# Where a fast matrix product's sums are made: on GpSimd beside the up projection, or on VectorE in other stages

## The chip, the cores and the metric

The kernel runs on one core of a Trainium2 chip. The metric is the device time of one execution in microseconds (us). A core has TensorE (PE, matmuls; its weight loads are shown as PEld), VectorE (DVE), ScalarE (ACT), GpSimd (POOL) and SyncE (SP), whose queue issues all of this kernel's DMAs.

## The reference, cut to what matters

One decoder layer over 16 + 1024 tokens of width 1024: a token mixer (latent attention and a Mamba-2 state-space mixer, gated and summed), then a gated MLP; each is followed by a layer norm.

```python
mixed = sigmoid(g_attn) * y_attn + sigmoid(g_ssd) * y_ssd
h = layer_norm(ALPHA * h + mixed @ w_out, ln1_g, ln1_b)
u = causal_dwconv(h @ w_up, conv_w, conv_b)      # width 3; D_FF = 2816
gate, val = split(u, 2)
h = layer_norm(ALPHA * h + (silu(gate) * val) @ w_down, ln2_g, ln2_b)
```

All inputs and the output are float32.

## The kernel before, in words

Every matrix product is made of three matmuls in a rounded float32 format: an operand is split into a high part (a cast on ACT) and a low part (a subtraction on DVE, `split`, or the same two lines in `load_w`), and high x high, low x high and high x low are accumulated in PSUM. Weights come by DMA into `wraw` (two buffers of 512 KB) and are split into `wh` and `wl` (four buffers each in the pool that all stages share).

The stages that count here, in order of time:

- **Gates' stage** (pool `B3`, lines 666 to 762, about 540 to 720 us): 8 rounds; round m makes the attention's gate m (`gate`, with a DVE multiplication) and the attention's output projection (`o_proj`, ACT copies PSUM). In between lie `dt_chain` and `h_centered`, small work, mostly on DVE.
- **State-space mixer**, then the mixer's projections and `wout` for two halves of the tokens (514 columns each). The second half's sum of squares `ssq` ends this part.
- **Root**: `inv_root` (line 201) sums `ssq` over the partitions with ten matmuls against ones, makes the reciprocal root in a chain of twelve small DVE operations, and spreads the result with ten matmuls against the identity. With it, `normed` (line 996) normalises the second half, stores it, and lines 1052 to 1075 make the seven right-hand forms of the next stage: sums and differences of the two halves, each split.
- **Up projection** (lines 1078 to 1238): the product h @ w_up is cut 2 x 2, and each block f of 128 gate and 128 value columns (`NFF` = 22 blocks) takes seven products of a Strassen-Winograd scheme instead of eight; a product is 24 matmuls in `mm3h`. `wload` brings two weight tiles per block, `wrest` makes the sums s1 to s4 of their quarters on POOL and splits them. `conv_up` is the width-3 convolution on ACT and DVE. Products 1 and 2 need only the first half of the tokens, which is ready long before; so for the first four blocks (`NHEAD`) these "tops" are made first, while the second half is normalised. They need rhs 1 and 2, and the others need the forms: 6 needs T2, 7 T3, 5 T1, 3 B2, 4 T4.
- **`down_sums`** (line 1178): for the same scheme in the next stage, four sums of the quarters of w_down are needed. For each of 11 pairs of weight rows it loads two 512 KB tiles, makes four subtractions on POOL in place, and stores both tiles to DRAM (`t13_d`, `t42_d`). It is called in the loop over blocks 4 to 14, its tiles have one buffer each, and it reads nothing but an input.
- **Down projection** (lines 1242 to 1392): seven products of 132 matmuls with 512 columns, over 11 values of j. The left sides are tiles A11, A12, A21, A22 of the gated values, loaded back from DRAM; `left` makes the sums of products 7, 6, 5 and 3 on POOL, per j, when `forms` asks for that j. `forms` splits the left and the right side; seven sets of buffers hold what is split ahead. Products come in the order 1, 2, 7, 6, 5, 3, 4.

The order of instructions on each engine is fixed ahead of time by a list planner, which takes of the instructions that it reckons ready the one that stands first in the program; `tc.high_priority(n)` lets a block count as n instructions earlier, and `tc.issue_after(ins)` makes the block's instructions on the same engine queue behind `ins`. On the chip each engine runs its list in that order, and SP issues its DMAs in order, each when its semaphores allow it.

Of the kernel before, what the change touches and what calls it, by code (L numbers as in the profile page):

```python
# [103 lines left out]
def tile_hybrid(ctx: ExitStack, tc: tile.TileContext, x, vecs, consts, cos, sin, win, wqb, wk, wv,  # L104
# [79 lines left out]
    def mm3h(ps, lhs, rhs, start=True):  # L184

        n = len(lhs)
        for k in range(n):
            (ah, al), (bh, bl) = lhs[k], rhs[k]
            for i, (a, b) in enumerate(((ah, bh), (al, bh), (ah, bl))):
                for c0, c1 in HC:  # L190
                    nc.tensor.matmul(ps[:, PO + c0:PO + c1], a, b[:, c0:c1], start=(start and k == 0 and i == 0),  # L191
                                     stop=(k == n - 1 and i == 2), skip_group_check=not start)

    def half(ps):
        return ps[:, PO:PO + HN]
# [2 lines left out]
        nc.scalar.copy(H, src)  # L198
        nc.vector.tensor_sub(L, src, f32(H))  # L199

    def inv_root(ss, n, scale, eps):


        ps = ctile() if n <= 512 else dpair()
        groups = [(0, n)] if n <= 512 else HC
        starts = [a + min(j * P, b - a - P) for a, b in groups for j in range(-(-(b - a) // P))]
        k = len(starts)
        for j, o in enumerate(starts):
            nc.tensor.matmul(ps[:, j:j + 1], ss[:, o:o + P], ones[:, :1], start=True, stop=True)
# [6 lines left out]
        for j, o in enumerate(starts):  # L216
            e = o + P
            nc.tensor.matmul(res[:, done:e], r[:, j:j + 1].broadcast_to([P, P]), ident[:, done - o:],
                             start=True, stop=True)
            done = e  # L220
        return res

    def rsqrt_cols(r, v, t):
# [442 lines left out]
    with pool("B3", 1) as p3:  # L666
# [24 lines left out]
        def dt_chain():  # L691
# [5 lines left out]
            for c in range(3):  # L697
# [27 lines left out]
                for k in range(3):  # L725
                    nc.tensor.transpose(tp[:S, k * 64:(k + 1) * 64], q[:, k * S:(k + 1) * S], ident[:64, :64])
                nc.scalar.copy(tok[:, 3 * c:3 * c + 3, :], tp[:S, :192].rearrange("p (a b) -> p a b", b=64))
        def h_centered(c):

            n = C1[c] - lo(c)  # L730
            hfs = []
            for k in range(KT):
                hfs.append(p3.tile([P, 352], F32, name="hf", tag="hf", bufs=9))
                nc.sync.dma_start(hfs[k][:, :n], h_d[k][:, lo(c):C1[c]])
            sum_ = p3.tile([P, 352], F32, name="hs", tag="hf", bufs=9)
            for k in range(1, KT):
# [18 lines left out]
        for m in range(KT):  # L755
            gate(B_GA, m, m1_d, yat)
            if m == 2:
                dt_chain()
            if m > 2 and m - 3 < 3:
                h_centered(m - 3)  # L760
            if m + 3 < KT:
                o_proj(m + 3)
# [284 lines left out]
    pf2 = eF.enter_context(pool("F2", 40))  # L1047
    p0 = eF.enter_context(pool("E0", 1))
    pz = eD.enter_context(pool("Dz", hB, "right"))
    with tc.high_priority(400):  # L1050
        rd = inv_root(ssq, HN, 1.0 / D, LN_EPS)
    T1, T2, T3, T4, B2 = ([None] * hB for _ in range(5))
    b11 = []
    for j in range(hB):
        b11.append(ftile(pz, F32))
        nc.sync.dma_start(b11[-1], h1_d[j][:, cols(0)])
    t2 = []
    for j in range(hB):
        b12, b22 = normed(1, j, rs[j], rd), normed(1, j + hB, rs[j + hB], rd)
        nc.vector.tensor_sub(b11[j], b12, b11[j])  # L1060
        t2.append(dtmp("t2", "yl" if j < 3 else "ml", 3))
        nc.vector.tensor_sub(t2[j], b22, b11[j])
        T2[j] = form(pf2, t2[j])
    for j in range(hB):
        nc.vector.tensor_sub(rs[j], rs[j + hB], rs[j])
        T3[j] = form(pf2, rs[j])
    for j in range(hB):
        T1[j] = form(pf2, b11[j])
    for j in range(hB):
        B2[j] = form(pf2, rs[j + hB])  # L1070
    for j in range(hB):
        b21 = dtmp("b21", "r", 8)
        nc.sync.dma_start(b21, h1_d[j + hB][:, cols(0)])
        nc.gpsimd.tensor_sub(b21, b21, t2[j])
        T4[j] = form(pf2, b21)

    rhs = {1: B1[:hB], 2: B1[hB:], 3: B2, 4: T4, 5: T1, 6: T2, 7: T3}
    HW = hB * P

    def wsplit(pl, src, bufs):
# [15 lines left out]

    def wrest(f, w):

        with tc.high_priority(wprio[0]):
            a11, a12 = wload(f)
            a21, a22 = wload(f + NFF)

            s1, s2, s3, s4 = (p0.tile([P, 512], F32, name=k, tag=k) for k in ("s1", "s2", "s3", "s4"))
            nc.gpsimd.tensor_add(s1, a21, a22)
            nc.gpsimd.tensor_sub(s2, s1, a11)  # L1110
            nc.gpsimd.tensor_sub(s3, a11, a21)
            nc.gpsimd.tensor_sub(s4, a12, s2)
            r = {}
            if w is None:
                r.update({1: wsplit(wp, a11, 4), 2: wsplit(wp, a12, 4)})
            for q, a in ((4, a22), (7, s3), (6, s2), (5, s1), (3, s4)):
                r[q] = wsplit(p0, a, 4) if q in (7, 6, 3) else wsplit(pe[0], a, 3)
            return r

    def prod(ps, q, w, start=True):  # L1120
        mm3h(ps, w[q], rhs[q], start)

    pe = []

# [35 lines left out]
        st[f]["c11"] = etile("c11", NHEAD)  # L1160
        nc.scalar.copy(st[f]["c11"], half(st[f]["x0"]))

    for f in range(NHEAD):
        with tc.high_priority(300):
            tops[f] = wtop(f)
            q = st[f]
            q["x0"] = dpair()
            prod(q["x0"], 1, tops[f])
            q["p1"] = etile("p1", NHEAD)
            nc.scalar.copy(q["p1"], half(q["x0"]))  # L1170
            if f:
                second(f - 1)
            if f == NHEAD - 1:
                second(f)

    eD.close()
    pe.append(eF.enter_context(pool("E1", 1)))
    def down_sums(j):

        x, y = (pe[0].tile([P, D], F32, name=k, tag=k) for k in ("tw1", "tw2"))  # L1180
        nc.sync.dma_start(x, wdl[j])
        nc.sync.dma_start(y, wdl[j + KH])
        (b11, b12), (b21, b22) = ((t[:, :512], t[:, 512:]) for t in (x, y))
        nc.gpsimd.tensor_sub(b11, b12, b11)
        nc.gpsimd.tensor_sub(b12, b22, b12)
        nc.gpsimd.tensor_sub(b22, b22, b11)
        nc.gpsimd.tensor_sub(b21, b21, b22)
        nc.sync.dma_start(t13_d[j], x)
        nc.sync.dma_start(t42_d[j], y)

    first(0)
    begun = 1
    for f in range(NFF):
        q = st[f]
        if f >= NHEAD and f < NHEAD + KH:
            down_sums(f - NHEAD)
        while begun < min(NHEAD, f + 2):
            first(begun)
            begun += 1
# [43 lines left out]
    with pool("Er", 4) as pr, pool("Ea", 4) as pa_, pool("Eh0", 8) as ph0, pool("Eb", 40) as pb, \  # L1243
# [10 lines left out]
            return raw[i, j]  # L1254

        def left(q, j):
            if q in (1, 2, 4):
                return A({1: 11, 2: 12, 4: 22}[q], j)
            if q == 7:
                t = p.tile([P, 512], F32, name="s3", tag="s3", bufs=3)  # L1260
                nc.gpsimd.tensor_sub(t, A(11, j), A(21, j))
                return t
            if q == 6:
                nc.gpsimd.tensor_add(A(21, j), A(21, j), A(22, j))
                nc.gpsimd.tensor_sub(A(11, j), A(21, j), A(11, j))
                return A(11, j)
            if q == 5:
                return A(21, j)
            nc.gpsimd.tensor_sub(A(12, j), A(12, j), A(11, j))
            return A(12, j)  # L1270
# [91 lines left out]
        for t in range(4):  # L1362
            add(t)
            nc.scalar.copy(u4[t], rp[t])
        product(1, x0, True, None, lambda t: nc.scalar.copy(p1[t], x0[t]))
        g2 = p.tile([P, D], F32, name="g2")
        b2 = p.tile([P, D], F32, name="b2")
        nc.sync.dma_start(g2, ln2[0:1].broadcast_to([P, D]))
# [1 line left out]

        x1 = banks(ctile)
        add = residual(0, 0, x1, True)
        product(2, x1, False, add, lambda t: nc.vector.tensor_add(p1[t], p1[t], x1[t]))
        x2 = banks(ctile)
        product(7, x2, True)
        product(6, x0, False, None, lambda t: nc.scalar.copy(u2[t], x0[t]))

        def c22(t):
            nc.vector.tensor_add(u4[t], u4[t], x0[t])
            nc.vector.tensor_add(u4[t], u4[t], x2[t])  # L1380
            nc.vector.bn_stats(bs[1][t][:, 1], u4[t])

        product(5, x0, False, None, c22)
        add = residual(0, 1, x0, False)
        product(3, x0, False, add, lambda t: norm2(0, t, (p1[t], x0[t]), (), (0, 1)))
# [104 lines left out]
```

## Time and profile before

| | us |
|---|---|
| runs | 2536.19, 2531.0, 2533.59 |
| median | 2533.59 |
| profiled execution, its own time | 2531.04 |
| its span, first to last instruction | 2529.3 |
| PE busy | 2403.9 (95%) |
| DVE busy | 1745.5 (69%) |
| ACT busy | 1136.7 (45%) |
| POOL busy | 336.8 (13%) |
| mean granted clock of PE | 0.977 |

Busy times of PE come from modelled ends, so a busy PE isn't always PE at its peak; the number of matmuls in a stretch is the surer measure. In a window's row there stand the stretch and its length, then for each engine the busy time and in brackets the count of instructions, the granted clock as a share of full speed, the share of DMA engines busy and the GB/s. A row of waits names who waited, at which line, for whom, the total, how often, and the longest. A row of the timeline gives start, duration, engine, line, operation, tiles, count, and in brackets the idle time before it and who ended it.

### The profile page before, as it was taken

The numbers are of one execution on the slowest core, as the hardware profiler recorded it, in microseconds if no ns is written. First come the engines' busy times: TensorE is split into PE (matmuls) and PEld (weight loads), VectorE is DVE, ScalarE is ACT, GpSimd is POOL, SyncE is SP. The second block draws the span as 40 slices with busy tenths as digits, with TensorE's granted clock in tenths as the row PEclk, the third lists the DMA queues.
The fourth block names the chain that finished last, engine by engine and source line by source line (L and its number), as shares of the span: only waits on it lengthen the run. The fifth ranks groups of instructions, "written<-read, shape, count | busy, mean of one in ns | idle before, by whom it ended". The sixth has DMA issues, their size and how long they took to land.

```text
span 2529.3 us, 42622 instructions
## 1 busy us (share of the span) xinstructions
PE 2403.9 (95%) x16319; PEld 2269.6 (90%) x16319; DVE 1745.5 (69%) x3857; ACT 1136.7 (45%) x2481; POOL 336.8 (13%) x278
## 2 busy tenths in 40 slices
PE   6999999999999999999999999998787999998896
PEld 6999899899999999999999999998787999997685
DVE  6467677684666777777777548547786777766558
ACT  6345455562245554555454323424433444444243
POOL 0000000000000000000000002011675222205504
PEclk9999999999999999999999999999798999999998
DMA  5121011152643212222221536543455222246232
GB/s 200 46 65 40 30 37 42 40 156 81 192 154 100 89 62 97 68 79 86 68 92 55 175 132 191 174 147 130 158 201 198 77 81 86 77 163 235 77 109 96
DMA packets 124620, 277.29 MB, mean 110 GB/s; under 512 B 14720, under 2 KB 49792, under 8 KB 122368
## 3 DMA queue, kind: packets, MB, share of 16 engines
q1 hardware_dynamic: 124416, 274.57, 33.0%
q8 instruction: 128, 2.10, 0.3%
q14 instruction: 76, 0.62, 0.1%
HBM read 209.62 MB, written 62.80 MB: 108 GB/s over the span
## 4 chain that ended last, share of the span: by engine, by line
PE 78%; DVE 7%; POOL 4%; DMA 4%; issue 3%; ACT 2%; SPq 0%; DVEq 0%; POOLq 0%; ACTq 0%
PE d L191 21%; PE g L171 12%; PE g L173 12%; PE g L172 12%; PE g L1321 5%; PE c L607 3%; PE c L882 2%; PE c L906 1%; PE c L601 1%; PE c L886 1%; DMA yl<-y_d 1%; DMA tw<-wdl 1%; DVE f L199 1%; PE c L554 1%; PE c L556 1%
## 5 line engine op out<-in xcount | busy, mean ns | idle before, releaser
L191 PE MATMUL d<-f,wh 128*128 128x258 f32 (+1 forms) x4000 | 666.5, 289 | 44.5 <-ACT u L1219 9.1
L191 PEld LDWEIGHTS d<-f,wh 128*128 128x128 f32 x4000 | 569.1, 196 | 49.6 <-ACT wh L198 10.3
L171 PE MATMUL g<-h,wh 128*128 128x348 f32 (+3 forms) x1560 | 507.5, 325 | 4.7 <-ACT lat L389 4.7
L173 PE MATMUL g<-h,wh 128*128 128x348 f32 (+3 forms) x1560 | 506.3, 325 | 0.0
L172 PE MATMUL g<-h,wl 128*128 128x348 f32 (+3 forms) x1560 | 506.1, 325 | 0.0
L191 PE MATMUL d<-f,wl 128*128 128x258 f32 (+1 forms) x2000 | 412.0, 289 | 5.2 <-DVE wl L199 3.6
L191 PEld LDWEIGHTS d<-f,wl 128*128 128x128 f32 x2000 | 319.6, 196 | 6.6 <-DVE wl L199 4.4
L161 DVE TENSOR_TENSOR wl<-wraw,wh 128x512 fp32r<-128x512 f32 (+2 forms) x278 | 193.7, 698 | 161.9 <-ACT wh L160 159.2
L171 PEld LDWEIGHTS g<-h,wh 128*128 128x128 f32 x1560 | 294.7, 189 | 7.6 <-ACT lat L389 5.0
L172 PEld LDWEIGHTS g<-h,wl 128*128 128x128 f32 x1560 | 295.0, 189 | 2.5 <-issue 2.4
L173 PEld LDWEIGHTS g<-h,wh 128*128 128x128 f32 x1560 | 294.3, 189 | 2.4 <-issue 2.4
L160 ACT CAST wh<-wraw 128x512 fp32r<-128x512 f32 (+2 forms) x278 | 167.3, 605 | 252.8 <-PE d L191 126.5
L199 DVE TENSOR_TENSOR wl<-wraw,wh 128x512 fp32r<-128x512 f32 x136 | 119.0, 884 | 74.3 <-ACT wh L198 74.3
L171 PE MATMUL g<-a,wh 128*128 128x348 f32 (+2 forms) x456 | 148.8, 327 | 1.6 <-DVE kn L199 1.1
L172 PE MATMUL g<-a,wl 128*128 128x348 f32 (+2 forms) x456 | 147.3, 323 | 0.0
L173 PE MATMUL g<-a,wh 128*128 128x348 f32 (+2 forms) x456 | 147.2, 323 | 0.0
L198 ACT CAST wh<-wraw 128x512 fp32r<-128x512 f32 x136 | 82.4, 618 | 120.6 <-DMA wraw<-wup 60.5
L787 DVE SCALAR_TENSOR_TENSOR xc<-g,V,xc 128x347 f32<-128x347 f32 (+2 forms) x180 | 103.7, 576 | 38.9 <-ACT xc L783 36.0
L1134 DVE SCALAR_TENSOR_TENSOR va<-u,V,va 128x512 f32<-128x512 f32 x88 | 99.9, 1135 | 20.9 <-ACT va L1132 19.5
L1321 PE MATMUL g<-wh,dh 128*128 128x512 f32 x352 | 112.4, 401 | 1.5 <-ACT wh L198 1.5
L872 ACT ACTIVATE G<-ac,tok 116x116 f32<-116x116 f32 x288 | 91.8, 380 | 42.7 <-PE c L882 42.7
L793 POOL MEMSET xc<- 128x4 f32 x20 | 2.0, 102 | 787.2 <-DVE y L919 454.1
(308 smaller groups left out, 4389.0 us busy)
## 6 DMA issues: line engine op xcount, KB each, us to landing
wraw<-win SPq DMA_DIRECT2D x65, 512.0 KB, 3.4
wraw<-wup SPq DMA_DIRECT2D x48, 512.0 KB, 3.7
ac<-cs_d SPq DMA_DIRECT2D x16, 1044.0 KB, 5.8
wraw<-wos SPq DMA_DIRECT2D x32, 512.0 KB, 3.9
tw<-wdl SPq DMA_DIRECT2D x22, 512.0 KB, 4.1
t_d<-tw SPq DMA_DIRECT2D x22, 512.0 KB, 2.8
gv<-gv_d SPq DMA_DIRECT2D x44, 256.0 KB, 5.6
wraw<-t_d SPq DMA_DIRECT2D x44, 256.0 KB, 3.2
```

The source lines that it names most:

```text
L160: nc.scalar.copy(h[:, :n * ncol], r)
L161: nc.vector.tensor_sub(l[:, :n * ncol], r, f32(h[:, :n * ncol]))
L171: nc.tensor.matmul(ps, ah, bh, start=(k == 0), stop=False)
L172: nc.tensor.matmul(ps, al, bh, start=False, stop=False)
L173: nc.tensor.matmul(ps, ah, bl, start=False, stop=(k == n - 1))
L191: nc.tensor.matmul(ps[:, PO + c0:PO + c1], a, b[:, c0:c1], start=(start and k == 0 and i == 0), stop=(k == n - 1 and i == 2), skip_group_c ...
L198: nc.scalar.copy(H, src)
L199: nc.vector.tensor_sub(L, src, f32(H))
L787: nc.vector.scalar_tensor_tensor(t[:, l:n], ps[:, hal + l - s:hal + n - s], vec("cw", (3 - s) * 24 + ct), t[:, l:n], ALU.mult, ALU.add)
L872: nc.scalar.activation(G_[:, k * S:(k + 1) * S], ac[:S, hh, C0[b] + k * S:C0[b] + (k + 1) * S], AF.Relu, bias=tok[:, 3 * b + k, 32 + hd:33 ...
L1134: nc.vector.scalar_tensor_tensor(t, src[:, 2 - k:HN - k], vec("fw", (2 - k) * 44 + ti), t, ALU.mult, ALU.add)
L1321: nc.tensor.matmul(pss[t], a[:, o], b, start=(first and j == 0 and i == 0), stop=(j == KH - 1 and i == 2), skip_group_check=not first)
```

## The change

Four edits. `mm3h` and `prod` return their last matmul, so that others can be queued behind it.

1. `down_sums` moves into the gates' stage (two calls in each of rounds 1 to 5, one in round 6), its tiles into that stage's pool, and its four subtractions from POOL to DVE.
2. The definitions of the up projection move ahead of the root, and the tops' products are issued around it: product 1 of block 0, the root's ten sums, product 1 of block 1, the root's ten spreading matmuls, product 2 of blocks 0 and 1, then blocks 2 and 3. The forms of the second half come behind all tops in the program. The priority of 400 on the root and of 300 on the tops is gone.
3. `wrest` has the priority 100 instead of 400 for the first four blocks.
4. The left sides of products 7, 6, 5 and 3 are made by `sums` on DVE, each for all j, in place (A21 becomes A11 - A21, then A22 minus that, A11 becomes the sum of A21 and A11, A12 becomes A12 - A21); the loads of all A tiles stand ahead of them in the program, without `forms`' priority.

```diff
+    def inv_root(ss, n, scale, eps, after=None, between=None):
...
+        with tc.issue_after(after.ins) if after else ExitStack():
+            for j, o in enumerate(starts):
+                ins = nc.tensor.matmul(ps[:, j:j + 1], ss[:, o:o + P], ones[:, :1], start=True, stop=True)
+        if between:
+
+            with tc.issue_after(ins.ins):
+                after = between()
...
+        with tc.issue_after(after.ins) if between else ExitStack():
+            for j, o in enumerate(starts):
...
+        root_end[0] = ins.ins
         return res
...
+        def down_sums(j):
+
+            x, y = (p3.tile([P, D], F32, name=k, tag=k) for k in ("tw1", "tw2"))
+            nc.sync.dma_start(x, wdl[j])
+            nc.sync.dma_start(y, wdl[j + KH])
+            (b11, b12), (b21, b22) = ((t[:, :512], t[:, 512:]) for t in (x, y))
+            nc.vector.tensor_sub(b11, b12, b11)
+            nc.vector.tensor_sub(b12, b22, b12)
+            nc.vector.tensor_sub(b22, b22, b11)
+            nc.vector.tensor_sub(b21, b21, b22)
+            nc.sync.dma_start(t13_d[j], x)
+            nc.sync.dma_start(t42_d[j], y)
...
             if m == 2:
                 dt_chain()
+            for j in range(2 * m - 2, 2 * m):
+                if 0 <= j < KH:
+                    down_sums(j)
...
-    with tc.high_priority(400):
-        rd = inv_root(ssq, HN, 1.0 / D, LN_EPS)
...
+        with tc.high_priority(100 if w else wprio[0]):
...
+    rd = inv_root(ssq, HN, 1.0 / D, LN_EPS, top(0), lambda: top(1))
+    with tc.issue_after(root_end[0]):
+        second(0)
+    second(1)
+    for f in range(2, NHEAD, 2):
+        top(f)
+        top(f + 1)
+        second(f)
+        second(f + 1)
...
-        if f >= NHEAD and f < NHEAD + KH:
-            down_sums(f - NHEAD)
...
         def left(q, j):
-            if q in (1, 2, 4):
-                return A({1: 11, 2: 12, 4: 22}[q], j)
-            if q == 7:
-                t = p.tile([P, 512], F32, name="s3", tag="s3", bufs=3)
-                nc.gpsimd.tensor_sub(t, A(11, j), A(21, j))
-                return t
...
+            return A({1: 11, 2: 12, 7: 21, 6: 21, 5: 11, 3: 12, 4: 22}[q], j)
+
+        def sums(q):
+
+
+            for j in range(KH):
+                if q == 7:
+                    nc.vector.tensor_sub(A(21, j), A(11, j), A(21, j))
+                elif q == 6:
+                    nc.vector.tensor_sub(A(21, j), A(22, j), A(21, j))
+                elif q == 5:
+                    nc.vector.tensor_add(A(11, j), A(21, j), A(11, j))
+                else:
+                    nc.vector.tensor_sub(A(12, j), A(12, j), A(21, j))
...
+        for j in range(KH):
+            A(11, j)
         product(1, x0, True, None, lambda t: nc.scalar.copy(p1[t], x0[t]))
+        for j in range(KH):
+            A(12, j)
...
+        for i in (21, 22):
+            for j in range(KH):
+                A(i, j)
+        sums(7)
         product(2, x1, False, add, lambda t: nc.vector.tensor_add(p1[t], p1[t], x1[t]))
         x2 = banks(ctile)
         product(7, x2, True)
+        sums(6)
+        sums(5)
         product(6, x0, False, None, lambda t: nc.scalar.copy(u2[t], x0[t]))
...
+        sums(3)
         product(5, x0, False, None, c22)
```

## Rows read from the trace of the kernel before

**Rows 1.** The page's forty slices of 63 us, busy tenths.

```profile
PE   6999999999999999999999999998787999998896
POOL 0000000000000000000000002011675222205504
```

**Rows 2.** Windows: PE, PEld, DVE, ACT, POOL busy, clock, DMA share, GB/s.

```profile
540.00:720.00 180.00, 179.47 (x1138) 177.90 (x1137) 104.49 (x208) 54.08 (x117) 0.31 (x3) 1.00 0.52 164
1734.30:1742.50 8.20, 3.51 (x21) 3.44 (x21) 3.98 (x15) 1.25 (x2) 0.00 (x0) 0.70 0.20 64
1742.50:1770.00 27.50, 24.86 (x194) 24.22 (x193) 26.55 (x37) 17.52 (x30) 6.02 (x4) 0.96 0.44 154
1770.00:1867.00 97.00, 72.46 (x475) 69.00 (x476) 77.83 (x86) 37.56 (x61) 65.04 (x42) 0.84 0.51 179
1867.00:1961.80 94.80, 77.91 (x584) 76.74 (x583) 65.95 (x70) 32.31 (x54) 59.31 (x39) 0.91 0.54 189
1961.80:2253.30 291.50, 291.50 (x2400) 291.31 (x2400) 220.65 (x288) 140.71 (x228) 71.59 (x52) 0.99 0.26 82
2253.30:2262.50 9.20, 6.08 (x49) 5.86 (x48) 6.69 (x12) 7.32 (x13) 0.00 (x0) 1.00 1.02 343
2262.50:2328.00 65.50, 63.77 (x276) 51.61 (x277) 37.40 (x44) 31.48 (x58) 20.71 (x14) 0.95 0.78 268
2328.00:2384.10 56.10, 42.16 (x154) 31.40 (x154) 38.69 (x34) 15.49 (x28) 46.66 (x31) 0.85 0.20 66
2384.10:2508.50 124.40, 124.40 (x558) 101.51 (x557) 80.58 (x160) 52.62 (x95) 22.23 (x17) 1.00 0.32 105
```

**Rows 3.** Waits of POOL and of ACT from 1835 to 1965 us.

```profile
POOL tw L1184 <- DMA tw<-wdl: 28.8, 6, 7.1
ACT wh L198 <- DMA wraw<-wup: 25.0, 3, 11.0
```

**Rows 4.** Waits of ACT from 2328 to 2384 us.

```profile
ACT dh L198 <- POOL s L1261: 34.8, 7, 12.2
```

**Rows 5.** Timeline from 1725 to 1850 us: the root, DVE's start, POOL's.

```profile
1736.61 1.34 PE L209 MATMUL d<-ones,ssq 128*128 128x1 f32 x10 [2.27 <-DVE ssq L1044]
...
1740.38 2.47 PE L218 MATMUL d<-K,ir 128*128 128x128 f32 x10 [2.43 <-DVE ir L230]
...
1742.89 2.07 DVE L997 SCALAR_TENSOR_TENSOR r<-r,V,d 128x514 f32<-128x514 f32 x3 [2.65 <-PE d L218]
...
1763.98 1.48 POOL L1109 TENSOR_TENSOR s<-wraw 128x512 f32<-128x512 f32 x1 [44.37 <-DMA wraw<-wup]
```

**Rows 6.** Groups of POOL: down_sums' costliest line, the left sides' cheapest.

```profile
L1185 POOL TENSOR_TENSOR tw<-tw,tw 128x512 f32<-128x512 f32 x11 | 19.1, 1736 | 9.1 <-DMA tw<-wdl 8.8
...
L1261 POOL TENSOR_TENSOR s<-gv 128x512 f32<-128x512 f32 x11 | 15.8, 1444 | 76.9 <-DMA gv<-gv_d 68.2 <-DVE dh L199 8.7
```

**Rows 7.** The page's DMA issues: count, KB each, us to landing.

```profile
wraw<-win SPq DMA_DIRECT2D x65, 512.0 KB, 3.4
...
tw<-wdl SPq DMA_DIRECT2D x22, 512.0 KB, 4.1
t_d<-tw SPq DMA_DIRECT2D x22, 512.0 KB, 2.8
```

**Rows 8.** Groups of DVE, 1770 to 1962 us, then 1962 to 2253 us.

```profile
L199 DVE TENSOR_TENSOR wl<-s,wh 128x512 fp32r<-128x512 f32 x33 | 37.6, 1146 | 9.9 <-ACT wh L198 9.5
L1134 DVE SCALAR_TENSOR_TENSOR va<-u,V,va 128x512 f32<-128x512 f32 x26 | 34.1, 1313 | 5.1 <-ACT va L1132 4.7
...
L1134 DVE SCALAR_TENSOR_TENSOR va<-u,V,va 128x512 f32<-128x512 f32 x58 | 62.8, 1082 | 13.7 <-ACT va L1132 12.7
L199 DVE TENSOR_TENSOR wl<-s,wh 128x512 fp32r<-128x512 f32 x55 | 37.9, 688 | 4.8 <-ACT wh L198 3.2
```

**Rows 9.** Gates' stage: a split in DVE's timeline; SP's longest wait.

```profile
610.16 0.69 DVE L161 TENSOR_TENSOR wl<-wraw,wh 128x512 fp32r<-128x512 f32 x1 [8.35 <-ACT wh L160]
...
SPq L147 <- DVE wl L161: 72.4, 16, 10.5
```

More of the change, by code (lines that the diff above doesn't have):

```diff
@@ L190, in mm3h @@
                 for c0, c1 in HC:
-                    nc.tensor.matmul(ps[:, PO + c0:PO + c1], a, b[:, c0:c1], start=(start and k == 0 and i == 0),
+                    ins = nc.tensor.matmul(ps[:, PO + c0:PO + c1], a, b[:, c0:c1], start=(start and k == 0 and i == 0),
                                      stop=(k == n - 1 and i == 2), skip_group_check=not start)
+        return ins
     def half(ps):
@@ L199, in split @@
         nc.vector.tensor_sub(L, src, f32(H))
-    def inv_root(ss, n, scale, eps):
+    root_end = [None]
+    def inv_root(ss, n, scale, eps, after=None, between=None):
         ps = ctile() if n <= 512 else dpair()
@@ L207, in inv_root @@
         k = len(starts)
-        for j, o in enumerate(starts):
-            nc.tensor.matmul(ps[:, j:j + 1], ss[:, o:o + P], ones[:, :1], start=True, stop=True)
+        with tc.issue_after(after.ins) if after else ExitStack():
[4 more added lines that the diff above has]
+                after = between()
         v, r, t = (sm.tile([P, 5], F32, name=nm, tag=nm) for nm in ("iv", "ir", "it"))
@@ L215, in inv_root @@
         done = 0
[L216 to L220, printed above, removed]
+        with tc.issue_after(after.ins) if between else ExitStack():
+            for j, o in enumerate(starts):
+                e = o + P
+                ins = nc.tensor.matmul(res[:, done:e], r[:, j:j + 1].broadcast_to([P, P]), ident[:, done - o:],
+                                       start=True, stop=True)
+                done = e
+        root_end[0] = ins.ins
         return res
@@ L1049, in tile_hybrid @@
     pz = eD.enter_context(pool("Dz", hB, "right"))
-    with tc.high_priority(400):
-        rd = inv_root(ssq, HN, 1.0 / D, LN_EPS)
[L1052 to L1082, printed above, removed]
+    rhs = {1: B1[:hB], 2: B1[hB:]}
     HW = hB * P
@@ L1102, in wrest @@
     def wrest(f, w):
-        with tc.high_priority(wprio[0]):
+        with tc.high_priority(100 if w else wprio[0]):
             a11, a12 = wload(f)
@@ L1120, in prod @@
     def prod(ps, q, w, start=True):
-        mm3h(ps, w[q], rhs[q], start)
+        return mm3h(ps, w[q], rhs[q], start)
     pe = []
@@ L1161, in second, with top @@
         nc.scalar.copy(st[f]["c11"], half(st[f]["x0"]))
[L1163 to L1174, printed above, removed]
+    def top(f):
+        tops[f] = wtop(f)
+        q = st[f]
+        q["x0"] = dpair()
+        ins = prod(q["x0"], 1, tops[f])
+        q["p1"] = etile("p1", NHEAD)
+        nc.scalar.copy(q["p1"], half(q["x0"]))
+        return ins
@@ new lines, in tile_hybrid @@
+    rd = inv_root(ssq, HN, 1.0 / D, LN_EPS, top(0), lambda: top(1))
[7 more added lines that the diff above has]
+        second(f + 1)
+    T1, T2, T3, T4, B2 = ([None] * hB for _ in range(5))
+    b11 = []
+    for j in range(hB):
+        b11.append(ftile(pz, F32))
+        nc.sync.dma_start(b11[-1], h1_d[j][:, cols(0)])
+    t2 = []
+    for j in range(hB):
+        b12, b22 = normed(1, j, rs[j], rd), normed(1, j + hB, rs[j + hB], rd)
+        nc.vector.tensor_sub(b11[j], b12, b11[j])
+        t2.append(dtmp("t2", "yl" if j < 3 else "ml", 3))
+        nc.vector.tensor_sub(t2[j], b22, b11[j])
+        T2[j] = form(pf2, t2[j])
@@ L1176, in tile_hybrid @@
+    for j in range(hB):
+        nc.vector.tensor_sub(rs[j], rs[j + hB], rs[j])
+        T3[j] = form(pf2, rs[j])
+    for j in range(hB):
+        T1[j] = form(pf2, b11[j])
+    for j in range(hB):
+        B2[j] = form(pf2, rs[j + hB])
+    for j in range(hB):
+        b21 = dtmp("b21", "r", 8)
+        nc.sync.dma_start(b21, h1_d[j + hB][:, cols(0)])
+        nc.gpsimd.tensor_sub(b21, b21, t2[j])
+        T4[j] = form(pf2, b21)
+    rhs.update({3: B2, 4: T4, 5: T1, 6: T2, 7: T3})
     eD.close()
@@ L1177, in tile_hybrid @@
     pe.append(eF.enter_context(pool("E1", 1)))
[L1178 to L1189, printed above, removed]
@@ L1256, in left @@
         def left(q, j):
-            if q in (1, 2, 4):
-                return A({1: 11, 2: 12, 4: 22}[q], j)
-            if q == 7:
-                t = p.tile([P, 512], F32, name="s3", tag="s3", bufs=3)
-                nc.gpsimd.tensor_sub(t, A(11, j), A(21, j))
-                return t
[L1263 to L1270, printed above, removed]
+            return A({1: 11, 2: 12, 7: 21, 6: 21, 5: 11, 3: 12, 4: 22}[q], j)
[9 more added lines that the diff above has]
+                    nc.vector.tensor_sub(A(12, j), A(12, j), A(21, j))
         def right(q, j):
```

## The prediction

> **What bounds the kernel now.** The forty slices of the page come first [rows 1]. TensorE (PE) is at nine tenths or more almost everywhere, so only a stretch where PE is not full can shorten the kernel. There are two such stretches behind the start-up: slices 27 to 30 (1710 to 1960 us) and 36 to 37 (2276 to 2400 us). In both GpSimd (POOL) has its only large busy shares, and nowhere else is PE that thin for so long.
>
> The second view cuts these stretches at the places that the change touches [rows 2]. [...] A price per matmul turns each row into lost time. From 1961.8 to 2253.3 us the up projection runs undisturbed: 2400 matmuls in 291.5 us, 0.1215 us each. By that price:
> - 1734.3 to 1742.5: no product at all, 8.2 us (the root of the second half's norm).
> - 1742.5 to 1770: 192 product matmuls (194 with two of the root's) need 23.3 of 27.5 us; 4.2 lost.
> - 1770 to 1867: 475 need 57.7 of 97.0; 39.3 lost.
> - 1867 to 1961.8: 584 need 70.9 of 94.8; 23.9 lost.
>
> In the down projection the row from 2384.1 on is undisturbed: 558 instructions, of which 32 are the transposes of two residuals; 124.4 / 526 = 0.236 us per matmul, transposes included. The 154 of 2328 to 2384.1 need 36.4 of 56.1; 19.7 lost.
>
> The third view says who is late. From 1835 on the sums of down_sums wait for their loads on POOL, and beside them the up projection's weights come late: ScalarE (ACT) waited 25.0 us for them in three waits [rows 3]. From 2328 to 2384 ACT waits 34.8 us for POOL's difference s3, the left side of product 7 [rows 4].
>
> **The change part by part.**
>
> *Root.* Now PE stands 2.27 us until the sum of squares is there and 2.43 us during the small VectorE (DVE) chain; the root's own 20 matmuls take 1.34 + 2.47 us [rows 5]. After the change the product of block 0 stands before the sums and that of block 1 inside the chain. Each is 24 x 0.1215 = 2.9 us, longer than the gap it fills. The sums start when the first product ends, 1734.3 + 2.9 = 1737.2 instead of 1736.6, and the normalisation starts at about 1742.8, as now (1742.89). So PE is 5.8 us of products ahead, but DVE, which starts its work on the second half there, gains nothing. That matters: in 1742.5 to 1770 DVE is busy 26.55 of 27.5 us, and it stays the late engine until the forms of the second half are made. By itself I count this part at 0 to 6 us, inside the next term. What else it gives: wraw has two buffers, and with two products done earlier, the last tops are split earlier (about 1750 instead of 1760), so block 0's second weight tile, whose arrival lets POOL begin at 1763.98 [rows 5], is there up to 10 us sooner. The lower priority of wrest (100 for 400) puts the forms before the weights of blocks 1 to 3, which is the order in which PE needs them.
>
> *down_sums leaves the up projection.* It takes away 44 POOL operations (1736 ns in the costliest of their four lines [rows 6]), and 22 loads and 22 stores of 512 KB [rows 7]. What stays (four sums per block, all splits) is what 1961.8 to 2253.3 also has, and there PE waits for nothing that lasts. So the 23.9 us after 1867 go entirely. Before 1867 DVE sets the end. It is busy 26.55 + 77.83 = 104.4 us from 1742.5 to 1867. Part of this is DVE held up while POOL works: from 1770 to 1962 the splits of sums take 1146 ns and the conv steps 1313 ns, later 688 and 1082 [rows 8]; 33 x 0.458 + 26 x 0.231 = 21 us, about half of it before 1867. DVE then needs 104.4 - 10.6 = 93.8 us and is done at 1836; with a little idle time I take 1838, against 1867 now: 29 us. What is late next is DVE, with the forms and then the conv of blocks 0 to 3; about 20 us of PE's waiting stay. Bounds of this term: if PE alone set it, 667 matmuls from 1737.3 on (root's 3 us counted) end at 1818, 49 us; if DVE stays as slow as now and only its idle time of 97.0 - 77.8 = 19 us shrinks by two thirds, 13 us. Term: 29 + 24 = 53 us, from 37 to 73.
>
> *down_sums in the gates' stage.* It adds 44 DVE subtractions. None stands there now; the nearest row is a split of the same 128x512 shape at 0.69 us [rows 9], so 44 x 0.69 = 30 us, on a DVE that is busy 104.5 of 180 us [rows 2]. PE is full there, so anything that delays a weight costs at once. The cover is depth: the 8.35 us of idle before that split are DVE's wait for ACT, which itself waits for PE to give a buffer back, and SP waits 72.4 us in 16 waits for wraw to come free, so weights are split about a whole product (180 us for 16 products, 11 us) before use, and loaded (3.4 us [rows 7]) before that. Four subtractions are 2.8 us. The 23 MB of traffic over 180 us are 128 GB/s on top of 164, below the 343 GB/s reached in 9 us at 2253; the tile pair has one buffer, so each set waits for the last one's stores and the sets spread by themselves. Bounds: nothing (less is excluded, as PE is full at the upper clock there) and 30 us, if DVE's time came out in full. I take 1 us, near the lower end, because DVE has 75 us free and needs 30.
>
> *Left sides on DVE.* Also 44 operations: on POOL 1444 ns each in the cheapest of their four lines [rows 6], on DVE 690 by the same row as above. In 2328 to 2384 POOL's queue is what PE waits for [rows 4], so it goes, and the DVE splits beside it get shorter. DVE's budget per product is 22 splits (15.1 us) plus at most 22 sums (15.1), against 31 us of PE time; on average 22 splits and 6.3 sums with the additions, some 23 us. It fits, with product 7 and 5 tight. New waits: a sum of product 6 overwrites what product 7's split reads, but that split is made ahead of its product, so the sum has 20 us or more. Loading all of A21 and A22 before product 2 brings nothing forward that matters: DMA is at 0.20 from 2328 on. Bounds: 0 (DVE as late as POOL was) and 19.7 plus what 2262.5 to 2328 has above its 244 matmuls, 65.5 - 57.6 = 7.9, part of which are transposes that stay [rows 2]. I take 20, by the row in which the wait stands.
>
> **Sum.** 53 + 20 - 1 = 72 us off the profiled execution's 2531.0 us (span 2529.3 and 1.7 around it): 2459 us. The median shown is 2533.6, 2.6 above; I leave the number at 2459.
>
> **Rivals.**
> 1. *The head is PE's, not DVE's.* If the earlier weights and the freed DVE keep PE fed from 1770 on, the first term is 73 instead of 53: 2439 us. For it: the splits are ready earlier. Against: DVE at 26.55 of 27.5 us before any down_sums begins.
> 2. *DVE takes POOL's place.* The head gives 13 only (2475), or the sums in the down projection make splits as late as POOL did (2479), or both (2495). For it: DVE runs near 0.9 in the head, and it is one queue in order. Against: DVE at 220.65 of 291.5 us where PE is full, so 76% is bearable.
> 3. *Slower: the gates' stage starves.* A subtraction whose tile has not landed stands at the head of DVE's queue, and the weight splits behind it wait; the stores behind SP's wait hold the weight loads in the same way. The present trace has this on POOL: six waits of tw for wdl, 28.8 us in all, 7.1 the longest [rows 3]. Per set that is a store, two loads and four sums, about 2.8 + 4.1 + 4.1 + 2.8 = 14 us at most [rows 7] against a cover of 11; 3 us x 11 sets cost 33, still faster. It decides where a set holds DVE for more than 11 + 73 / 11 = 17.6 us; at 20 us a set it costs 9 x 11 = 99 against the other terms' 73, and the time is 2557. Against: SP and DMA are half idle there.
>
> [...]
>
> **How the numbers follow.** Forecast 0.64; rival 1 0.13; rival 2 0.17; rival 3 0.03 slower, and 0.03 for a gates' stage or a head that gives nearly everything back (half of it within 0.2%, about 5 us, what a measurement of this kernel can tell from no change; a sixth slower). So faster 0.95, same 0.015, slower 0.035. The range reaches from rival 1 to the worse half of rival 2: 2436 to 2492.
>
> **What would show it.** Right: no tw on POOL behind 1700; DVE near full from 1742 to about 1838 and PE then without waits at 0.1215 us a matmul until the up projection ends near 2207; the first down product follows as now; no wait of ACT for POOL in the down projection; the gates' stage still 180 us. Wrong: PE waits for wh or wl in the gates' stage; PE waits after 1840 in the up projection; DVE at 95% with PE waiting in products 7 to 5.

## The result, and the profile after

The changed kernel takes 2476.43 us (median of 4 runs, 2472.53 to 2480.07) against 2534.43 of the kernel before in the same runs (2531.0 to 2536.19): ratio 0.9773, 95% interval [0.9754, 0.9791]. The forecast was 2459 us with a range of 2436 to 2492: faster, as said, by 58 us instead of 72. The profiled execution took 2476.96 us (span 2474.9).

The slices after, the lines that answer to [rows 1] (62 us each): counted from 0, as in the prediction, and apart from the first and the last, PE is thin only in slices 28 and 29 (1732 to 1856 us), and POOL keeps little.

```profile
PE   6999999999999999999999999999789999999996
...
POOL 0000000000000000000000000202332222210004
```

The windows, columns as in [rows 2], of the gates' stage, the root, the work on the second half, PE's new wait, the rest of the head, the rest of the up projection, the step to the down projection, and the down projection:

```profile
540.00:720.00 180.00, 174.37 (x1078) 172.21 (x1077) 120.28 (x231) 51.76 (x113) 0.30 (x3) 0.97 0.79 262
1748.05:1756.70 8.65, 8.65 (x75) 8.57 (x74) 5.11 (x18) 3.47 (x6) 0.00 (x0) 1.00 0.19 63
1756.70:1779.00 22.30, 20.86 (x168) 20.13 (x166) 21.85 (x31) 15.44 (x26) 6.52 (x4) 1.00 0.45 166
1779.00:1794.00 15.00, 0.03 (x1) 0.06 (x1) 12.79 (x18) 8.78 (x16) 10.18 (x4) 0.51 0.24 71
1794.00:1870.00 76.00, 64.47 (x478) 62.12 (x479) 60.22 (x78) 30.90 (x48) 29.01 (x20) 0.94 0.25 84
1870.00:2234.00 364.00, 363.16 (x3004) 362.61 (x3002) 274.88 (x359) 178.09 (x289) 88.67 (x64) 1.00 0.27 86
2234.00:2242.00 8.00, 7.64 (x42) 6.53 (x43) 6.95 (x12) 4.22 (x9) 0.00 (x0) 1.00 0.73 244
2242.00:2448.00 206.00, 206.00 (x918) 167.74 (x917) 144.03 (x259) 95.82 (x174) 17.99 (x14) 1.00 0.48 159
```

Where the 54.4 us of span went, between the same points in both traces (the first is where the last product ahead of the root ends; block 0's first top follows there at once in the changed kernel, and behind the root in the kernel before):

| stretch | before | after | difference | forecast |
|---|---|---|---|---|
| start to the end of that product | 1734.3 | 1748.05 | +13.8 | +1 |
| from there to the up projection's last product | 525.8 | 485.8 | -40.0 | -53 |
| from that to the down projection's last matmul | 249.4 | 221.3 | -28.1 | -20 |
| the rest | 19.8 | 19.8 | 0 | 0 |

The gates' stage shows its loss first in the waits from 540 to 790 us (engine, line, what it waited for: us in all, times, longest). They are small ones of PE, for the few matmuls of the scan chain, of the centring and at the start of the next stage (ct), and beside them VectorE's waits for the sums' loads:

```profile
PE c L736 <- DVE q L733: 3.6, 2, 3.4
PE c L762 <- DVE hs L760: 2.1, 1, 2.1
PE c L858 <- DVE ct L817: 1.7, 1, 1.7
...
DVE tw L745 <- DMA tw<-wdl: 10.6, 7, 3.4
DVE tw L744 <- DMA tw<-wdl: 9.0, 7, 3.4
```

The timeline shows how the two hang together. The subtraction of L744 stood 2.20 us for its tile, the centring's addition of L760 came right behind it in VectorE's list, and PE stood 2.06 us for that addition. PE's 3.36 us for q, up to 636.92, has the same order ahead of it: two waits for tw of 3.37 and 1.67 us at 624.10 and 627.06, then the scan chain's operations.

```profile
706.32 0.69 DVE L744 TENSOR_TENSOR tw<-tw 128x512 f32<-128x512 f32 x1 [2.20 <-DMA tw<-wdl]
706.93 0.51 DVE L760 TENSOR_TENSOR hs<-hs,hf 128x344 f32<-128x344 f32 x1
...
707.59 1.49 PE L762 MATMUL c<-hs,ones 128*128 128x344 f32 x2 [2.06 <-DVE hs L760]
```

PE's waits are 7.4 us together, less than the stage lost. Behind each of the two longest the clock was lower too: the granted clock was 0.50 from 636.5 to 640.5 us and 0.58 from 707.6 to 711.6, and a matmul took some 0.29 us there instead of 0.16.

The head of the up projection in the timeline (start, length, engine, line, what, idle before and its releaser). The root's matmuls stand without a gap, unlike [rows 5]; later, from 1778 us on, PE waits 15.73 us, and the end of that wait is the end of a chain through T4: load of `b`, POOL's four differences, their splits, u2.

```profile
1751.16 1.17 PE L213 MATMUL d<-ones,ssq 128*128 128x1 f32 x10
1755.24 1.35 PE L227 MATMUL d<-K,ir 128*128 128x128 f32 x10
...
1756.69 2.07 DVE L1023 SCALAR_TENSOR_TENSOR r<-r,V,d 128x514 f32<-128x514 f32 x3
...
1781.67 10.18 POOL L1205 TENSOR_TENSOR b<-b,t 128x514 f32<-128x514 f32 x4 [7.81 <-DMA b<-h_d]
...
1787.95 5.28 DVE L200 TENSOR_TENSOR f<-b,f 128x514 fp32r<-128x514 f32 x4 [1.81 <-ACT f L199]
1793.14 0.68 DVE L1148 TENSOR_TENSOR u<-p,d 128x514 f32<-128x514 f32 x1
...
1793.97 0.77 PE L191 MATMUL d<-f,wh 128*128 128x258 f32 x2 [15.73 <-DVE u L1148]
```

In the down projection ACT no longer waits for POOL, as in [rows 4], but for PE: the splits are ahead.

```profile
ACT dh L199 <- PE g L1339: 45.3, 8, 9.0
ACT dh L199 <- PE c L1339: 31.4, 6, 7.7
```

### The profile page after: what moved, and what is told of

It reads as the page before. It is cut to its first block, busy times and chain, and to the rows that moved or that the text cites. A ratio compares the mean times of both kernels' runs of the same rounds, so it can differ in the third digit from the quotient of the medians.

```text
span 2474.9 us, 42581 instructions
## 1 busy us (share of the span) xinstructions
PE 2379.6 (96%) x16319; PEld 2252.3 (91%) x16319; DVE 1746.3 (71%) x3945; ACT 1137.5 (46%) x2481; POOL 202.2 (8%) x190
## 4 chain that ended last, share of the span: by engine, by line
PE 80%; DVE 8%; DMA 6%; issue 2%; ACT 2%; POOL 1%; SPq 0%; DVEq 0%; ACTq 0%; POOLq 0%
PE d L191 25%; PE g L171 11%; PE g L173 11%; PE g L172 11%; PE g L1339 5%; PE c L617 3%; PE c L1339 2%; PE c L908 2%; PE c L611 1%; PE c L932 1%; PE c L912 1%; DMA yl<-y_d 1%; DMA tw<-wdl 1%; DMA wraw<-wup 1%; DVE wl L161 1%
## 5 line engine op out<-in xcount | busy, mean ns | idle before, releaser
L191 PE MATMUL d<-f,wh 128*128 128x258 f32 (+1 forms) x4000 | 655.5, 286 | 28.2 <-DVE u L1148 15.7
L191 PEld LDWEIGHTS d<-f,wh 128*128 128x128 f32 x4000 | 558.7, 192 | 31.0 <-ACT wh L199 20.0
L191 PEld LDWEIGHTS d<-f,wl 128*128 128x128 f32 x2000 | 314.4, 192 | 7.9 <-DVE wl L200 5.5
L200 DVE TENSOR_TENSOR wl<-wraw,wh 128x512 fp32r<-128x512 f32 x136 | 99.6, 741 | 60.3 <-ACT wh L199 60.2
L1133 DVE SCALAR_TENSOR_TENSOR va<-u,V,va 128x512 f32<-128x512 f32 x88 | 94.8, 1077 | 20.4 <-ACT va L1131 19.1
L199 ACT CAST wh<-s 128x512 fp32r<-128x512 f32 x88 | 53.9, 617 | 88.2 <-PE d L191 45.6
```

The lines of the kernel that those rows point to most:

```text
L191: ins = nc.tensor.matmul(ps[:, PO + c0:PO + c1], a, b[:, c0:c1], start=(start and k == 0 and i == 0), stop=(k == n - 1 and i == 2), skip_g ...
L1133: nc.vector.scalar_tensor_tensor(t, src[:, 2 - k:HN - k], vec("fw", (2 - k) * 44 + ti), t, ALU.mult, ALU.add)
```

## Experiments

Each run stands beside runs of the kernel before on the same chip (2530.8 to 2532.8 us); the changed kernel's ratio is 0.9773. Three kernels take the change apart, made from the kernel before. In the edits `...` marks lines left out.

**Left sides alone.**

```diff
...
-                nc.gpsimd.tensor_sub(t, A(11, j), A(21, j))
...
+                    nc.vector.tensor_sub(A(21, j), A(11, j), A(21, j))
...
+        sums(7)
...
```

> The kernel before with only the left sides of the down projection made on VectorE, in place. My reading of the two traces: from the up projection's last matmul to the down projection's last one the change took 28 us out (249 to 221), all of it POOL's queue, so this alone gives 2534 - 28 = 2506 us. Rival (the forecast's term): VectorE takes part of it back, 20 us, 2514. If the 28 us came partly from the loads that begin earlier in the up projection without down_sums, it is under 20.

Measured 2505.22 against 2531.42: 0.9891 [0.9876, 0.9906], 26.2 us. From the up projection's last product to the last down product it takes 203.1 instead of 230.3 us: -27.2, nearly all of the changed kernel's -28.1. PE's longest wait in the stage is 1.4 us.

**Sums of w_down alone**, in the gates' stage and on VectorE.

```diff
...
+                if 0 <= j < KH:
+                    down_sums(j)
...
-            down_sums(f - NHEAD)
...
```

> The kernel before with only down_sums moved into the gates' stage, on VectorE. Theory: the gates' stage loses 10 to 12 us and the stage behind it 2, as in the changed kernel; the up projection gains the 24 us behind 1867 and 10 to 15 before: 2534 + 13 - 37 = 2510 us. Rival: the head of the up projection is held by the second half's forms whatever POOL does, so only the 24 come: 2523.

Measured 2508.1: 0.9907 [0.9892, 0.9922], 23.3 us. From the normalisation's first operation to the up projection's end it takes 479.5 instead of 516.1 us (-36.6; 476.1 in the changed kernel), and the normalisation starts 11.7 us later. So the stage that gives is the up projection and the stage that pays lies ahead of it.

**The root's order alone**, with the weights' priority of 100.

```diff
...
+    rd = inv_root(ssq, HN, 1.0 / D, LN_EPS, top(0), lambda: top(1))
+    with tc.issue_after(root_end[0]):
+        second(0)
...
```

> The kernel before with only the root's matmuls between the first products and wrest's lower priority. Theory: PE gets ahead by two products and then waits for the same VectorE chain (forms, then u2 of block 0), so the time moves by less than 5 us: 2529 to 2534. Rival: PE's 6 to 8 us at the root stay gained: 2527. Second rival: with down_sums still on POOL in the head, the lower priority of wrest lets them go first and the time rises by 5.

Measured 2527.77: 0.9986 [0.9976, 0.9995], 3.7 us. The three parts sum to 53.2 us; the whole gave 58.0, or 54.1 between the two profiled executions. The trace puts none of the 3.7 us where the edit works: from the normalisation's first operation to the up projection's end it takes 517.8 us against 516.1. The normalisation starts 2.1 us earlier, most of it won ahead of the root, and the down projection, which the edit leaves as it is, is 2.9 us shorter.

This kernel, with the sums of w_down still on POOL, has the same long wait of PE in the head as the changed kernel, with the same chain through T4 ahead of it:

```profile
1778.12 0.77 PE L191 MATMUL d<-f,wh 128*128 128x258 f32 x2 [15.73 <-DVE u L1132]
```

With the sums moved and the old order (the run before this one) no wait of PE from 1730 to 2250 us is over 5.8 us. So the long wait comes with the new order of tops and forms, whether or not the sums are in the head.

**The changed kernel without the sums.** It leaves out the loads, subtractions and stores; the down projection reads quarters of w_down in their place.

```diff
...
-                if 0 <= j < KH:
-                    down_sums(j)
...
```

> The changed kernel without down_sums at all (products 4 to 7 of the down projection read w_down itself in place of its sums; the same bytes are read there). This measures the whole price of the sums in the gates' stage. Theory: it is the 11 us that PE loses in that stage and some 2 behind it: 2476 - 13 = 2463 us. Rival: the offset that the traces show is the plan's and not the sums', then 2470 to 2476. Forecast's own term: 1 us, 2475.

Measured 2463.6: 0.9734 [0.9715, 0.9754]. The sums cost 12.8 us where they now stand by the medians, 9.9 by the ratios; in the trace the normalisation starts 12.1 us earlier without them, and PE's waits from 540 to 790 us are 0.8 us instead of 7.4. The next runs ask why.

**The subtractions on GpSimd again, still in the gates' stage.**

```diff
-            nc.vector.tensor_sub(b11, b12, b11)
...
+            nc.gpsimd.tensor_sub(b11, b12, b11)
...
```

> The changed kernel with the four subtractions of down_sums in the gates' stage on GpSimd, everything else as it is; loads, stores and SP's queue are the same. Theory (queue): VectorE's list holds subtractions that wait for their tiles, the small chains of dt_chain and h_centered stand behind them, and PE stands at its small matmuls for these chains; with the subtractions on GpSimd VectorE is free and 8 to 11 us come back: 2466 us. [...]

Measured 2497.94: 0.9864 [0.9843, 0.9885], 21 us worse than the changed kernel: a miss. VectorE no longer stands at the sums, but SP does: one of these stores is in line right ahead of the scan chain's last load `xx`, which went out 0.4 us behind it, at 646.0 us, though its buffer had been free since 633. The waits from 540 to 790 us:

```profile
SPq L748 <- POOL tw L745: 39.8, 10, 5.6
...
PE c L736 <- DVE q L733: 16.6, 2, 12.4
...
ACT u L713 <- DMA xx<-dt_d: 18.6, 3, 10.0
```

**The scan chain and the centring ahead of the sums**, by priority.

```diff
-                dt_chain()
+                with tc.high_priority(300):
+                    dt_chain()
...
```

> The changed kernel with dt_chain and h_centered 300 instructions earlier in the planner's order. Queue theory: if the order on VectorE is what holds PE's small matmuls, 3 to 8 us come back, 2471; but a subtraction that the plan believes ready and that waits for its tile still blocks, so not all. Rival (traffic): no change, 2476.

Measured 2476.65: 0.9784 [0.9765, 0.9803], no change. VectorE's waits for tw stayed (13.9 + 7.3 us), and so did PE's (4.1 us for q, 3.1 for xc, 2.5 for ct): the loss only moved. The run does not decide between VectorE's queue and DMA traffic, since it left the waits in place.

**The sums' transfers from GpSimd's queue instead of SP's.**

```diff
-            nc.sync.dma_start(x, wdl[j])
...
+            nc.gpsimd.dma_start(x, wdl[j])
...
```

> The changed kernel with the four transfers of each gates' stage sum (two loads of w_down's row blocks, two stores of the differences) issued from GpSimd's queue instead of SP's. Queue theory: what the sums cost in the gates' stage (12.8 us when they are left out) is mostly that their stores stand in SP's queue until VectorE has made the differences, and hold the scan chain's own loads behind them (with the differences on GpSimd, SP waited 39.8 + 17.7 us for them and the whole got 21 us slower). Then SP's waits for tw are gone and 8 to 11 us come back: about 2467. Rival: the cost is VectorE's, which waits about 20 us at the head of its queue for the loads of tw and does 11 us of subtractions; then nothing comes back: 2474 to 2478.

Measured 2496.28: 0.9863 [0.9841, 0.9884], 20 us worse. SP's waits for tw are gone, and no time came back with them. That doesn't clear SP's queue in the changed kernel, because VectorE's waits doubled at the same time. Why they doubled is open: in POOL's queue both loads of a set stand behind both stores of the set before, which wait for VectorE, but in SP's queue they did so too in nearly every set, and VectorE's planned order differs between the two kernels. In VectorE's list the rest of the scan chain's second third stood behind four sets of sums, and every wait moved it: its last operation came at 657.3 us instead of 636.5, PE waited 17.3 us for it, and the chain's next load `xx`, whose buffer it frees, went out at 655.1 instead of 634.9. The waits from 540 to 790 us:

```profile
DVE tw L744 <- DMA tw<-wdl: 28.8, 7, 8.0
...
DVE tw L745 <- DMA tw<-wdl: 11.2, 8, 4.0
...
PE c L736 <- DVE q L733: 19.0, 2, 17.3
...
ACT u L713 <- DMA xx<-dt_d: 32.5, 3, 18.5
```

PE made 12 matmuls in the worst 20 us, at a granted clock of 0.60:

```profile
640.00:660.00 20.00, 2.71 (x12) 2.30 (x11) 14.95 (x32) 1.60 (x4) 3.70 (x7) 0.60 0.60 211
```

Two runs ask what ends the 15.7 us wait in the up projection's head; one more tries to fill it, and one undoes a priority.

**u2 of block 0 outside pool E1.**

```diff
...
-            q["u2"] = etile("u2", 2)
-            nc.vector.tensor_add(q["u2"], q["p1"], half(q["x0"]))
+            q["u2"] = etile("u2", 2) if f else tokf.rearrange("p a b -> p (a b)")[:, :HN]
+            with tc.high_priority(150):
+                nc.vector.tensor_add(q["u2"], q["p1"], half(q["x0"]))
```

> The changed kernel with u2 of block 0 in a tile of its own (the space of tok, which is dead by then) and its addition 150 instructions earlier, so that it no longer follows the four T4 forms on VectorE. Theory (memory): PE's one long wait, 15.7 us before product 5 of block 0, is for u2, whose tile lies where T4's sources lie; without that PE waits some 5 us there, and 5 to 9 us come back: 2469 us. Rival: the block's weights and VectorE's load decide; the wait moves to the next products and the time stays within 3 us of 2476.

Measured 2476.96: 0.978 [0.9762, 0.9798], no change, a miss. u2 was made 13.7 us earlier and PE waited as long, now for product 5's weights. These lie in E1 too, and ACT made them right behind T4's last cast, while the weights of 7, 6 and 3, which lie in E0, had long been split.

```profile
1793.07 0.80 PE L191 MATMUL d<-f,wh 128*128 128x258 f32 x2 [15.96 <-ACT wh L199]
...
1779.49 0.68 DVE L1150 TENSOR_TENSOR tok<-p,d 128x514 f32<-128x514 f32 x1
```

**T4 without its load and its difference.** T4 is made of another operand; all products are still made.

```diff
-        nc.sync.dma_start(b21, h1_d[j + hB][:, cols(0)])
-        nc.gpsimd.tensor_sub(b21, b21, t2[j])
-        T4[j] = form(pf2, b21)
+        T4[j] = form(pf2, t2[j])
```

> The changed kernel with T4 formed of t2 itself, without the second load of b21 and GpSimd's difference (T4 has other values than it should; all products are still made). Space theory: TensorE's wait of 15.7 us in the up projection's head ends when the space under pool E1 comes free, that is when T4's four forms, which read b21 in that space, are done at 1793.1; without b21 the last forms end some 6.5 us earlier, and the wait falls by as much: about 2470. Rival: the end of the wait is set by something else (the weights of block 0, the sums s1 to s4 on GpSimd), and the time stays within 1.5 us of 2476.5.

Measured 2467.02: 0.9746 [0.9726, 0.9767]. PE's wait ends with the chain, 4.5 us shorter; `ga` is one more tile of E1 that follows T4's splits:

```profile
1785.18 0.77 PE L191 MATMUL d<-f,wh 128*128 128x258 f32 x2 [11.26 <-ACT ga L1131]
```

From the normalisation to the stage's end it takes 471.5 instead of 476.1 us: 4.6 of the gain are the chain's. The other 4.4 came ahead of it (the normalisation starts at 1753.1 instead of 1757.5), in stages whose code the edit leaves as it is; so a change of 4 us in a total is not proof of a cause in this kernel, and the stage's own length has to be looked at.

**Product 7 ahead of product 5.**

```diff
...
-        prod(x0, 5, w, False)
...
+            with tc.issue_after(p7.ins):
+                prod(x0, 5, w, False)
...
```

> The changed kernel with product 7 of the eight head blocks issued on TensorE ahead of product 5. Both need nothing of pool E1 but product 5 adds onto the PSUM pair that u2 has still to be read from, and u2 and product 5's weights lie in E1. Then product 6 of block 1 and product 7 of block 0, 48 matmuls of about 0.121 us, run in the time of the 15.7 us wait: it falls by up to 5.8 us, about 2471. Rival: the wait is only moved (product 7's right side or its weights come as late as E1's space, or the eight later blocks pay it back): within 1.5 us of 2476.5.

Measured 2483.16: 0.9808 [0.9788, 0.9828], 7 us worse; neither forecast held. By the code and the trace, the list now had block 1's product 6 ahead of both, and its weights come through the two `wraw` buffers only when block 0's are split. PE stood there longer than before:

```profile
1799.77 1.01 PE L191 MATMUL d<-f,wh 128*128 128x258 f32 x3 [24.75 <-ACT wh L199]
```

**The weights' priority back at its old value.**

```diff
-        with tc.high_priority(100 if w else wprio[0]):
+        with tc.high_priority(wprio[0]):
```

> The changed kernel with wrest's priority of 400 for the first four blocks, as before. Theory: the splits of later blocks' sums go ahead of the second half's forms on VectorE, the forms are done later, and the up projection's head loses 3 to 8 us: 2481. Rival: the lower priority changes nothing, since the weights of block 1 can't be split before block 0's buffers are free: 2476.

Measured 2477.11: 0.9778 [0.9753, 0.9802], no change.

**Sums in the convolutions' stage, with three pairs of buffers, and half of T4's differences on VectorE**: a version to beat both.

```diff
...
-            for j in range(2 * m - 2, 2 * m):
-                if 0 <= j < KH:
-                    down_sums(j)
...
+                if ti < KH:
+                    down_sums(ti)
...
-        nc.gpsimd.tensor_sub(b21, b21, t2[j])
+        (nc.gpsimd if j < 2 else nc.vector).tensor_sub(b21, b21, t2[j])
```

> The changed kernel with the sums of w_down moved out of the gates' stage into the convolutions' stage behind it (one per channel tile, three pairs of buffers instead of one), where VectorE is busy 0.75 and the DMA share is 0.25 instead of 0.8; and two of T4's four differences on VectorE instead of GpSimd. The queue theory as the runs so far leave it: the gates' stage lost 12.8 us because VectorE's in-order queue stood at subtractions whose loads were late (10.6 + 9.0 us at tw) with the scan chain's operations behind them. In the quiet stage the loads land in some 2.5 us and the buffers are free long before, so the gates' stage gets 11 to 13 us back and the convolutions lose 0 to 4; the head's long wait ends some 3 us earlier: about 2463. Rival: 44 subtractions cost PE the same wherever they stand, since VectorE is as busy here as there: then the convolutions lose 10 us or more, and it is 2472 to 2478.

Measured 2466.68 against 2532.75: 0.9744 [0.9731, 0.9757], better than the changed kernel by 7 us going by the ratios and 10 by the medians. The gates' stage is full, and the convolutions' stage stays so from 800 us on with the sums in it. In the waits from 540 to 900 us VectorE's 19.6 us at tw are 1.1:

```profile
DVE tw L790 <- DMA tw<-wdl: 1.1, 1, 1.1
```

```profile
540.00:640.00 100.00, 99.87 (x636) 99.23 (x635) 55.88 (x110) 35.41 (x79) 0.00 (x0) 1.00 0.39 123
640.00:740.00 100.00, 99.61 (x630) 98.67 (x629) 53.68 (x107) 31.31 (x72) 0.30 (x3) 1.00 0.58 192
740.00:800.00 60.00, 58.38 (x406) 55.25 (x405) 52.19 (x123) 32.71 (x79) 0.30 (x3) 1.00 0.76 255
800.00:1100.00 300.00, 299.77 (x2062) 283.94 (x2061) 234.50 (x577) 158.35 (x379) 0.98 (x11) 1.00 0.32 108
```

The normalisation starts 10.6 us earlier, 1.5 us later than with no sums at all. That speaks for VectorE's waits as the cause, and against the subtractions themselves: the same 44 subtractions cost PE 1.5 us where the loads are there in time. It does not part the traffic from the queues, as both are eased, and the scan chain and the centring no longer stand beside the sums. The sums' loads took 4.5 us to land in the median (2.6 to 9.5; 4.6 in the changed kernel), not the 2.5 expected. The head's half gave nothing: PE's long wait fell to 14.42 us, but from the normalisation to the up projection's end it took 477.2 us against 476.1.

## Why the prediction was right, and which terms were off

**Root (0 to 6, inside the next term): right as to the gap and as to DVE.** The normalisation starts 8.64 us after the last product ahead of the root (8.59 before), and PE has no gap at the root. What PE won there it lost again: the part alone gave 3.7 us, none of it in this stage.

**Up projection (-53, measured -40).** The half behind 1867 was right: 3004 matmuls in 364 us, 0.1212 each, so the 23.9 us went whole, and DVE's operations beside POOL got shorter as said. In 1870 to 2234 the conv steps and the splits of sums take 1081 and 704 ns, where the first part of [rows 8] had 1313 and 1146:

```profile
L1133 DVE SCALAR_TENSOR_TENSOR va<-u,V,va 128x512 f32<-128x512 f32 x72 | 77.8, 1081 | 19.2 <-ACT va L1131 17.9
L200 DVE TENSOR_TENSOR wl<-s,wh 128x512 fp32r<-128x512 f32 x68 | 47.9, 704 | 5.9 <-ACT wh L199 4.6
```

The head was the term that was mis-sized: -29 forecast, -16 measured (-40 less the 23.9). The step is "about 20 us of PE's waiting stay". By 0.1215 us a matmul the 478 of 1794 to 1870 us need 58.1 of 76.0, so 17.9 are lost there, about as said: in waits of at most 2.2 us, 11.5 in all and mostly for DVE, which is busy 60.2 of the 76.0, and at a lower granted clock (0.94). But 15 us ahead of them, from 1779 to 1794, came on top. They are one chain, which the forecast did not follow and which the new order brings: T4's load, POOL's 10.18 us of differences, the last splits, and with them the space of E1, where u2 and product 5's weights lie. It cost PE 15.73 us, and the 24 matmuls of the 6 us that follow, part of the 17.9, ran at a granted clock of 0.52 (0.24 us each instead of 0.12, some 3 us more). That T4's end releases the wait is shown by its shift with the chain; that E1's space, and not merely the planned order, holds the weights back is read from the code and from which weights were late, and no run took E1 away from T4's sources.

**Gates' stage (+1, measured +12.8): mis-sized too.** The cover that I named was the right one for the weights, and held: PE never waited for a weight split there. What I left out was the other work in VectorE's line, the scan chain and the centring, whose few matmuls have no depth and stand in PE's list between full products. Rival 3 had the right head of VectorE's queue, but with weight splits behind it, and at 33 or 99 us instead of 12.8. In the trace, a subtraction waiting for its load held operations of these chains behind it (19.6 us of waits for tw in all). It held a ready operation too: the gate's multiplication of L698, whose two inputs ACT had written by 704.43 us, started at 707.36, behind the subtraction for which VectorE stood from 704.12 to 706.32 and the addition at 706.93. The totals go the same way: 40.0 us of such waits went with 20 us more lost (the transfers on GpSimd's queue), and 1.1 us with 1.5 us lost (the convolutions' stage). I reckoned with such a line for the weights alone; and [rows 3], on which rival 3 leans, show only that subtractions on POOL waited, not what stood behind them.

**Down projection (-20, measured -28.1).** Mechanism right, mis-sized by 8 us: it came out at about the upper bound of 27.6, so the 7.9 us that I left out, from 2262.5 to 2328, went too. DVE had the room: PE waits for no left side, and only 0.5 us at all from 2234 to 2460.

**Rivals.** PE-bound head: no, it lost 15 us to one wait and 17.9 behind it. DVE in POOL's place: in the down projection no, it hides the sums; in the head it was nearly full until 1786 us, but POOL's chain outlasted it. The time lies at that rival's first case (2475) by another cause.

**Luck.** The up projection and the gates' stage each came out some 13 us slower than forecast and the down projection 8 us faster, so the total came nearer to the forecast than its terms did. Without the 8 us it would still lie in the range.

## What to carry to other kernels

When work is moved to a stage that looks idle, ask of each engine's line what stands behind a waiting instruction, not only of the operands with depth; the small chains whose result PE takes next are what pays. Sums that read only inputs are worth trying where the DMA is quiet and buffers can be had several deep: the same operations cost 12.8 us in one stage and 1.5 in another, where traffic, buffers and neighbours had all changed. When products are moved ahead of the operations that feed the later ones, look where the wait goes: here the root's gaps closed and one wait of 15.7 us opened. And follow the next product's space as well as its inputs: a tile that waits for memory, as the code has it here, would show as a wait for the operation that writes it, as the 15.73 us for u2 may be.

## What the runs showed of the hardware that was not expected

In the last kernel's head, two VectorE subtractions took 1.76 and 1.75 us while POOL's took 2.5 each; the next VectorE one, with POOL idle, took 0.68:

```profile
1770.98 4.95 POOL L1204 TENSOR_TENSOR b<-b,t 128x514 f32<-128x514 f32 x2 [7.72 <-DMA b<-h_d]
...
1773.05 1.76 DVE L1204 TENSOR_TENSOR b<-b,t 128x514 f32<-128x514 f32 x1
1774.73 1.75 DVE L200 TENSOR_TENSOR f<-r,f 128x514 fp32r<-128x514 f32 x1
1776.41 0.68 DVE L1204 TENSOR_TENSOR b<-b,t 128x514 f32<-128x514 f32 x1
```

So dividing the four differences between the two engines took two off POOL's chain, but two of VectorE's operations beside POOL's took over twice as long (1.76 and 1.75 us against 0.68), and the stage gained nothing (477.2 against 476.1 us).
